# Residual adds ranked over weight tiles, a norm's scale asked for later, and split weights in half tiles: a change to a two-layer decoder trunk

## The chip, the cores and the metric

The kernel runs on one core of one Trainium2 chip. The core has five engines that run side by side: TensorE (PE in the profile; its weight loads are the row PEld), VectorE (DVE), ScalarE (ACT), GpSimd (POOL) and SyncE (SP), which issues most DMA transfers. The metric is the device time of one execution in microseconds, lower being better. The kernel before took 2509.03 us (median of three runs, 2508.16 to 2511.75).

## The reference

The program computes two residual layers over 256 positions of width 2048, in float32. The first layer mixes with a state-space part (SSD) and latent attention (MLA), the second with stick-breaking attention. Each is followed by a gated feed-forward network (FFN) with 5632 hidden columns.

```
def rms_norm(x, g):
    y = x * rsqrt(mean(x * x, axis=-1) + 1e-6)
    return y * g

def swiglu_ffn(h, w_gate, w_up, w_down):
    return (silu(h @ w_gate) * (h @ w_up)) @ w_down

for layer in range(2):
    h = rms_norm(x, mix_norm[layer])
    if layer % 2 == 0: mix = ssd_mla_mixer(h, w_in, ..., w_out)
    else:              mix = stick_breaking_mixer(h, w_qkv, w_out)
    x = x + mix
    x = x + swiglu_ffn(rms_norm(x, ffn_norm[layer]), w_gate[layer], w_up[layer], w_down[layer])
return rms_norm(x, final_norm)
```

All weights are read once from HBM, about 450 MB.

## The kernel before

**Products in three terms.** A float32 operand is split into a rounded part (hi, or wh for weights) and the rest (lo, wl). A product of 128 rows by 512 columns over 128 of K is three matmuls: hi by wh, hi by wl, lo by wh. `split` (L247 to L250) makes the two parts: ScalarE casts (L249), then VectorE subtracts (L250), so wl always comes after wh.

**Weights.** A raw weight tile `w` holds four K blocks of 512 columns (1 MB) and comes by one DMA or a few. `load_split` (L300) walks a weight matrix in groups of four K blocks: it loads the group, then splits it into `wh` and `wl`. Up to the fifth group the split is cut finer (`step`), then a group is one cast and one subtraction. `wh` and `wl` have two buffers each of their own (`whtile`, `wltile`, `wtile` with own=2); in the FFN every third one lies in a region of memory that the two kinds of layer share. Raw tiles have three buffers, and every fourth one in the FFN lies in that shared region.

**The shared region.** `region(kind)` closes the pool that is open and opens another over the same memory. In the attention layers ("acts") it holds 20 small tiles `s2x`, among them the attention outputs that the output projection reads. In the FFN ("sums") it holds one raw tile, two weight sums `wsum`, and one wh and one wl tile. A tile of the new pool waits for the tiles of the old pool that lie where it lies.

**Projections.** `project` (L333) runs all of K for 512 output columns and both tiles of 128 rows, with the matmuls at L340 to L342; K is 2048 in most, that is 16 blocks, four groups. `add_residual` (L390) then adds the result from PSUM to the residual `xres` on VectorE, one instruction per row tile (L395). PSUM has four accumulator banks, two per projection.

**The FFN.** `pair` (L467) computes 512 columns of gate and up together. Over the first half of K it forms seven products instead of eight, out of sums and differences of blocks: the weights' sums t1 to t4 (`wadd`, L464) are made on VectorE, and each of the seven weight operands b11, b22, t1, b21, t2, t4, t3 is then split. The products' matmuls are at L493, L494 and L498, in the order b11, b22, t1, b21, t2, t4, t3. Their left operands (`block_operands`) come from the residual's first two blocks of 512 columns. The second half of K is plain (L526 to L528, in `unit`) and reads the transposed third and fourth blocks. At its end `left` applies Silu, which needs the norm's scale `rstd`, and `right` multiplies. Eleven pairs come in groups of 2, 2, 2, 2, 3; each group is followed by four down projections.

**The norm.** The gain goes into the transposed operand, and the scale 1/rms is applied to results. `norm_block` and `operand_block` transpose one block of 512 columns of the residual on TensorE (L259, L413), finish the operands on ScalarE and VectorE (L268, L270), and square and sum. They run as tasks: a generator that yields counts of ticks; `tick` is called between groups of matmuls and advances those due. `join` runs a task to its end at once. `norm_end` (L383) joins all four blocks, then computes `rstd` by one reduction, six small VectorE instructions and a Sqrt on ScalarE. In `ffn` it is called at L572, ahead of the first pair.

**What sets the order.** TensorE runs in the order of the program text. The other engines' instructions are put in order by a planner that takes, of those ready in its own simulated time, the one with the lowest number; that order is then fixed, and each engine works through it. The default number is 10000000. Weight work counts up from 100000 (`wprio`), so earlier tiles come first, and `URGENT` is 50000. The residual adds have the default number.

The functions that the diff touches, and what calls them:

Of the kernel before, what the change touches and what calls it, by code (L numbers as in the profile page):

```python
# [8 lines left out]
F32 = mybir.dt.float32  # L9
# [6 lines left out]
P = 128  # L16
# [11 lines left out]
class Trunk:  # L28
# [6 lines left out]
    def __init__(self, ctx, tc, ins, out):  # L35
# [13 lines left out]
        self.banks = ["acc0", "acc1", "acc2", "acc3"]  # L49
        self.n, self.wn = 0, {}  # L50
        self.now, self.tasks = 0, []
# [36 lines left out]
    def region(self, kind):  # L88

        if self.shared is not None:  # L90
            self.shared.__exit__(None, None, None)
        self.shared, self.shared_kind = None, kind
        if kind:
            bufs = 20 if kind == "acts" else 2
            self.shared = self.tc.tile_pool(name=f"shared_{kind}", bufs=bufs, reuse_waits="tile")
            self.xp = self.shared.__enter__()
# [4 lines left out]

    def wtile(self, tag="w", dt=F32, bufs=4, own=3):

        n = self.wn[tag] = self.wn.get(tag, 0) + 1
        if self.shared_kind == "sums" and n % bufs == 0:
            return self.xp.tile([P, 4, 512], dt, name=self.nm(tag), tag=tag, bufs=1)
        return self.wp.tile([P, 4, 512], dt, name=self.nm(tag), tag=tag, bufs=own)

    def whtile(self):
        return self.wtile("wh", F32R, 3, 2)  # L110

    def wltile(self):
        return self.wtile("wl", F32R, 3, 2)

# [185 lines left out]
    def load_split(self, view, nk, n):  # L300

        nc = self.nc
        for k0 in range(0, nk, 4):
            k1 = min(nk, k0 + 4)
            res = []
            with self.priority(self.wprio):
# [5 lines left out]
                for ins in self.first if self.wprio <= 105000 else ():  # L312
                    order.enter_context(self.tc.issue_after(ins))
                wh, wl = self.whtile(), self.wltile()
                step = 1 if self.wprio < 102000 else 2 if self.wprio < 106000 else k1 - k0
                for c in range(0, k1 - k0, step):
                    d = c + step
                    self.split(wh[:, c:d, :n], wl[:, c:d, :n], w[:, c:d, :n])
                order.close()
                for k in range(k0, k1):  # L320
                    res.append((wh[:, k - k0, :n], wl[:, k - k0, :n]))
            yield from res
# [67 lines left out]
    def add_residual(self, ps, j, scale=None):  # L390
        nc, x = self.nc, self.xres
        for t in range(2):
            xs = x[:, t, j * 512:(j + 1) * 512]
            if scale is None:
                nc.vector.tensor_tensor(xs, ps[t], xs, op=ALU.add)  # L395
            else:
                nc.vector.scalar_tensor_tensor(xs, ps[t], scale[:, t:t + 1], xs, op0=ALU.mult, op1=ALU.add)

# [55 lines left out]
    def wsplit(self, w):  # L454
        wh, wl = self.whtile(), self.wltile()
        with self.priority(self.wprio):
            self.wprio += 100
            self.split(wh, wl, w)
        return wh, wl
# [90 lines left out]
    def ffn(self, layer, st, gain_next):  # L550
# [83 lines left out]
    def stick(self, st):  # L634
# [82 lines left out]
    def even(self, st):  # L717
# [58 lines left out]
        for n in range(4):  # L776
            ps = self.project(aT, self.cols(wo, n * 512, r0=SSD_W), KD)
            self.add_residual(ps, n)
            (self.operand_block if n < 2 else self.norm_block)(st, n, self.g_ffn[0])
        return st  # L780
# [345 lines left out]
```

## Time and profile before

| | us |
|---|---|
| median of three runs | 2509.03 (2508.16 to 2511.75) |
| the profiled execution's own time | 2512.09 |
| its span, first to last instruction | 2510.4 |
| TensorE busy | 2454.1 (98%) |
| VectorE busy | 1714.3 (68%) |
| ScalarE busy | 1298.1 (52%) |
| GpSimd busy | 130.9 (5%) |

The span is that of the one execution that the hardware profiler recorded; durations that are quoted come from it. A line of a timeline gives the start, the time, the engine, the line of the kernel, the operation, what is written and read, the shapes and the count; in brackets stands how long the engine was idle before it, and what ended that. A matmul of 512 columns shows some 0.39 us, but matmuls overlap and start some 0.23 us apart. The layers lie as follows: the first attention layer to 641 us, its FFN to about 1322, the stick-breaking layer to 1779, its FFN to the end.

### The profile page before, as it was taken

To read this page: it belongs to the slowest core of one execution; us is meant where nothing else is said; L and a number is where in the kernel's file an instruction comes from. 1 tells how busy PE (TensorE), PEld (TensorE's weight loads), DVE (VectorE), ACT (ScalarE), POOL (GpSimd) and SP (SyncE) were. 2 spreads that over 40 slices of the span, in tenths; PEclk is the share of its full clock that TensorE was granted. 3 is DMA by queue.
4 is the path that set the end of the run, shared out by engine and by line. 5 is a ranking of instruction groups with operands and counts; after the bars stand their busy time and mean duration, and the time that the engine had idled before them with its cause. 6 is when DMAs were issued, how large, how long until landed. Compare 5 with 4: busy or idle time off the path is not lost.

```text
span 2510.4 us, 27612 instructions
## 1 busy us (share of the span) xinstructions
PE 2454.1 (98%) x11176; PEld 2008.4 (80%) x11176; DVE 1714.3 (68%) x1476; ACT 1298.1 (52%) x1266; POOL 130.9 (5%) x164
## 2 busy tenths in 40 slices
PE   8999999999899999999999999999899999999998
PEld 7788877788688888888878787778688888888876
DVE  5775455456778778787965444445787878787874
ACT  6655555434554545454544545554554545454553
POOL 1231121000000000000000000000000000000001
PEclk9999999999899999999999999999999999999999
DMA  7654553355555556565554454445555656565653
GB/s 234 194 176 159 178 157 111 126 193 185 182 197 199 194 196 206 184 203 185 204 190 143 166 172 160 151 155 173 181 200 184 217 172 215 170 231 168 235 188 114
DMA packets 257824, 454.78 MB, mean 181 GB/s; under 512 B 20716, under 2 KB 45424, under 8 KB 257696
## 3 DMA queue, kind: packets, MB, share of 16 engines
q1 hardware_dynamic: 255168, 446.48, 53.1%
q0 software_dynamic: 1952, 5.48, 0.6%
q8 instruction: 88, 1.44, 0.2%
q10 hardware_dynamic: 576, 1.05, 0.1%
q14 instruction: 40, 0.33, 0.0%
HBM read 450.85 MB, written 2.13 MB: 180 GB/s over the span
## 4 chain that ended last, share of the span: by engine, by line
PE 56%; issue 39%; ACT 2%; DVE 1%; POOL 0%; DMA 0%; SPq 0%; POOLq 0%; ACTq 0%; DVEq 0%
PE acc L341 11%; PE acc L340 11%; PE acc L342 11%; PE acc L527 3%; PE acc L526 3%; PE acc L528 3%; PE acc L493 3%; PE acc L494 3%; PE acc L498 3%; PE tr L259 1%; ACT wh L249 1%; DVE wl L250 1%; PE at L1049 1%; PE at L978 1%; PE at L1048 0%
## 5 line engine op out<-in xcount | busy, mean ns | idle before, releaser
L250 DVE TENSOR_TENSOR wl<-w,wh 128x2048 fp32r<-128x2048 f32 (+2 forms) x431 | 966.3, 2250 | 578.3 <-ACT wh L249 569.5
L249 ACT CAST wh<-w 128x2048 fp32r<-128x2048 f32 (+2 forms) x431 | 807.3, 1875 | 732.5 <-PE acc L342 414.8
L340 PE MATMUL acc<-wh,s 128*128 128x512 f32 (+1 forms) x1728 | 692.2, 401 | 3.3 <-ACT wh L249 3.3
L341 PE MATMUL acc<-wl,s 128*128 128x512 f32 (+1 forms) x1728 | 673.6, 390 | 7.0 <-DVE wl L250 6.9
L342 PE MATMUL acc<-wh,s 128*128 128x512 f32 (+1 forms) x1728 | 674.2, 390 | 0.0
L341 PEld LDWEIGHTS acc<-wl,s 128*128 128x128 f32 x1728 | 326.2, 189 | 74.4 <-DVE wl L250 10.3
L342 PEld LDWEIGHTS acc<-wh,s 128*128 128x128 f32 x1728 | 325.3, 188 | 70.2
L340 PEld LDWEIGHTS acc<-wh,s 128*128 128x128 f32 x1728 | 325.9, 189 | 67.6 <-ACT wh L249 4.1
L528 PE MATMUL acc<-wl,s 128*128 128x512 f32 x704 | 275.3, 391 | 0.0
L527 PE MATMUL acc<-wh,s 128*128 128x512 f32 x704 | 275.2, 391 | 0.0
L526 PE MATMUL acc<-wh,s 128*128 128x512 f32 x704 | 275.2, 391 | 0.0
L493 PE MATMUL acc<-wh,s 128*128 128x512 f32 x616 | 246.4, 400 | 0.0
L494 PE MATMUL acc<-wh,s 128*128 128x512 f32 x616 | 242.4, 393 | 0.0
L249 ACT CAST wh<-wsum 128x2048 fp32r<-128x2048 f32 x66 | 125.9, 1910 | 84.6 <-PE acc L527 35.7
L498 PE MATMUL acc<-wl,s 128*128 128x512 f32 x616 | 166.1, 391 | 0.0
L250 DVE TENSOR_TENSOR wl<-wsum,wh 128x2048 fp32r<-128x2048 f32 x66 | 150.6, 2285 | 13.8 <-ACT wh L249 13.8
L527 PEld LDWEIGHTS acc<-wh,s 128*128 128x128 f32 x704 | 132.2, 188 | 29.1
L526 PEld LDWEIGHTS acc<-wh,s 128*128 128x128 f32 x704 | 132.2, 188 | 29.0
L528 PEld LDWEIGHTS acc<-wl,s 128*128 128x128 f32 x704 | 132.1, 188 | 29.0
L493 PEld LDWEIGHTS acc<-wh,s 128*128 128x128 f32 x616 | 116.9, 190 | 25.6
L494 PEld LDWEIGHTS acc<-wh,s 128*128 128x128 f32 x616 | 117.0, 190 | 24.3
L498 PEld LDWEIGHTS acc<-wl,s 128*128 128x128 f32 x616 | 115.8, 188 | 25.7
(246 smaller groups left out, 2063.3 us busy)
## 6 DMA issues: line engine op xcount, KB each, us to landing
w<-in_w_gate_dram SPq DMA_DIRECT2D x88, 1024.0 KB, 5.1
w<-in_w_up_dram SPq DMA_DIRECT2D x88, 1024.0 KB, 5.1
w<-in_w_down_dram SPq DMA_DIRECT2D x88, 1024.0 KB, 5.0
w<-in_w_qkv_dram SPq DMA_DIRECT2D x48, 1024.0 KB, 5.0
w<-in_w_in_dram SPq DMA_DIRECT2D x47, 1024.0 KB, 5.2
w<-in_w_out_even_dram SPq DMA_DIRECT2D x32, 1024.0 KB, 4.9
w<-in_w_out_odd_dram SPq DMA_DIRECT2D x16, 1024.0 KB, 5.0
w<-in_w_ukv_dram SPq DMA_DIRECT2D x32, 256.0 KB, 4.1
```

The source lines that it names most:

```text
L249: nc.scalar.copy(hi, src)
L250: nc.vector.tensor_tensor(lo, src, hi.bitcast(F32), op=ALU.subtract)
L259: self.nc.tensor.transpose(pt[:, k, t * P:(t + 1) * P], src(t, 2 * k2 + k), self.ident)
L340: nc.tensor.matmul(ps[t], hi[:, ts], wh, start=k == 0, stop=False)
L341: nc.tensor.matmul(ps[t], hi[:, ts], wl, start=False, stop=False)
L342: nc.tensor.matmul(ps[t], lo[:, ts], wh, start=False, stop=k == nk - 1)
L493: mm(ps, hi[:, k], wh[:, k], start=start and k == 0, stop=False, skip_group_check=True)
L494: mm(ps, lo[:, k], wh[:, k], start=False, stop=False, skip_group_check=True)
L498: mm(ps, hi[:, k], wl[:, k], start=False, stop=k == 3, skip_group_check=True)
L526: mm(ps, hi, wh, start=False, stop=False, skip_group_check=True)
L527: mm(ps, lo, wh, start=False, stop=False, skip_group_check=True)
L528: mm(ps, hi, wl, start=False, stop=stop, skip_group_check=True)
```

## The change

Three things are changed.

1. `add_residual` gives its VectorE instructions the number `URGENT`. The norm blocks of the third and fourth residual block after an output projection get that rank for their operands too.
2. `ffn` no longer calls `norm_end` ahead of the first pair. `left` calls it when it first needs the scale, at the end of that pair's plain part.
3. `wh` and `wl` lie in the shared region alone. In the FFN each has three buffers of four K blocks, as before in number. In the attention layers each has four buffers of two K blocks, and a group of four is split in two halves, each with its own cast and subtraction. Raw tiles stay as they were. The sizes in total are unchanged.

```
     def region(self, kind):
...
         if kind:
-            bufs = 20 if kind == "acts" else 2
-            self.shared = self.tc.tile_pool(name=f"shared_{kind}", bufs=bufs, reuse_waits="tile")
+            self.shared = self.tc.tile_pool(name=f"shared_{kind}", bufs=2, reuse_waits="tile")
             self.xp = self.shared.__enter__()
...
-    def wtile(self, tag="w", dt=F32, bufs=4, own=3):
-
-        n = self.wn[tag] = self.wn.get(tag, 0) + 1
-        if self.shared_kind == "sums" and n % bufs == 0:
-            return self.xp.tile([P, 4, 512], dt, name=self.nm(tag), tag=tag, bufs=1)
-        return self.wp.tile([P, 4, 512], dt, name=self.nm(tag), tag=tag, bufs=own)
-
-    def whtile(self):
-        return self.wtile("wh", F32R, 3, 2)
-
-    def wltile(self):
-        return self.wtile("wl", F32R, 3, 2)
+    def wtile(self):
+
+        self.wn += 1
+        pool, bufs = (self.xp, 1) if self.shared_kind == "sums" and self.wn % 4 == 0 else (self.wp, 3)
+        return pool.tile([P, 4, 512], F32, name=self.nm("w"), tag="w", bufs=bufs)
+
+    def part(self, tag):
+
+        nk, bufs = (2, 4) if self.shared_kind == "acts" else (4, 3)
+        return self.xp.tile([P, nk, 512], F32R, name=self.nm(tag), tag=tag, bufs=bufs)
...
                 for ins in self.first if self.wprio <= 105000 else ():
                     order.enter_context(self.tc.issue_after(ins))
-                wh, wl = self.whtile(), self.wltile()
-                step = 1 if self.wprio < 102000 else 2 if self.wprio < 106000 else k1 - k0
-                for c in range(0, k1 - k0, step):
-                    d = c + step
-                    self.split(wh[:, c:d, :n], wl[:, c:d, :n], w[:, c:d, :n])
+                np = 2 if self.shared_kind == "acts" else 4
+                for a in range(k0, k1, np):
+                    b = min(k1, a + np)
+                    wh, wl = self.part("wh"), self.part("wl")
+                    step = 1 if self.wprio < 102000 else np
+                    for c in range(0, b - a, step):
+                        d = min(c + step, b - a)
+                        self.split(wh[:, c:d, :n], wl[:, c:d, :n], w[:, a - k0 + c:a - k0 + d, :n])
+                    for k in range(a, b):
+                        res.append((wh[:, k - a, :n], wl[:, k - a, :n]))
                 order.close()
-                for k in range(k0, k1):
-                    res.append((wh[:, k - k0, :n], wl[:, k - k0, :n]))
...
             xs = x[:, t, j * 512:(j + 1) * 512]
-            if scale is None:
-                nc.vector.tensor_tensor(xs, ps[t], xs, op=ALU.add)
-            else:
-                nc.vector.scalar_tensor_tensor(xs, ps[t], scale[:, t:t + 1], xs, op0=ALU.mult, op1=ALU.add)
+            with self.priority(self.URGENT):
+                if scale is None:
+                    nc.vector.tensor_tensor(xs, ps[t], xs, op=ALU.add)
+                else:
+                    nc.vector.scalar_tensor_tensor(xs, ps[t], scale[:, t:t + 1], xs, op0=ALU.mult, op1=ALU.add)
...
     def wsplit(self, w):
-        wh, wl = self.whtile(), self.wltile()
+        wh, wl = self.part("wh"), self.part("wl")
...
         def left(t, c, s):
+            nonlocal rstd
+            if rstd is None:
+                rstd = self.norm_end(st)
             nc.vector.tensor_tensor(s, c, s, op=ALU.subtract)
...
             for n in range(n0, n0 + nb):
-                if rstd is None:
-                    rstd = self.norm_end(st)
                 self.pair(st, xT, self.cols(wg, n * 512), self.cols(wu, n * 512), left, right)
...
             self.add_residual(ps, n)
-            (self.operand_block if n < 2 else self.norm_block)(st, n, self.g_ffn[1])
+            if n < 2:
+                self.operand_block(st, n, self.g_ffn[1])
+            else:
+                self.norm_block(st, n, self.g_ffn[1], rank=self.URGENT)
```

The last hunk stands in `stick`; the same one stands in `even`, with `self.g_ffn[0]`.

More of the change, by code (lines that the diff above doesn't have):

```diff
@@ L49, in __init__ @@
         self.banks = ["acc0", "acc1", "acc2", "acc3"]
-        self.n, self.wn = 0, {}
+        self.n = self.wn = 0
         self.now, self.tasks = 0, []
@@ L778, in even @@
             self.add_residual(ps, n)
-            (self.operand_block if n < 2 else self.norm_block)(st, n, self.g_ffn[0])
+            if n < 2:
+                self.operand_block(st, n, self.g_ffn[0])
+            else:
+                self.norm_block(st, n, self.g_ffn[0], rank=self.URGENT)
         return st
```

## The prediction, made before the changed kernel was run

> **What bounds the kernel now.** I read the page's head first, then TensorE's waits, then the windows around the places where it waits, then the order of the instructions there.
>
> ```profile
> span 2510.4 us, 27612 instructions
> PE 2454.1 (98%) x11176; PEld 2008.4 (80%) x11176; DVE 1714.3 (68%) x1476; ACT 1298.1 (52%) x1266; POOL 130.9 (5%) x164
> ```
>
> TensorE is busy for 2454.1 of 2510.4 us; the change adds and removes no matmul, so all that it can win lies in the 56 us in which TensorE is idle, and in what such pauses cost afterwards. TensorE's waits say whom it waits for (us in total, times, longest):
>
> ```profile
> PE tr L259 <- DVE xres L395: 22.7, 2, 11.4
> PE acc L341 <- DVE wl L250: 8.7, 6, 1.8
> PE acc L340 <- ACT wh L249: 4.3, 5, 1.1
> ```
>
> The first row is two pauses of 11.4 us: transposes wait for a residual add. The next two, 13.0 us, are matmuls waiting for the two halves of a split weight tile. The windows around the two long pauses (first two rows), around the four worst waits for weights, all in the stick-breaking layer (next four), and of the two attention layers as a whole:
>
> ```profile
> core 0: us, PE busy (x) PEld busy (x) DVE busy (x) ACT busy (x) POOL busy (x), PEclk, DMA share, GB/s
> 638.00:662.00 24.00, 12.65 (x50) 10.05 (x49) 20.42 (x17) 10.84 (x15) 0.00 (x0) 0.72 0.42 141
> 1776.00:1800.00 24.00, 12.54 (x52) 10.00 (x51) 21.05 (x19) 11.36 (x15) 0.00 (x0) 0.79 0.41 143
> 1437.00:1450.00 13.00, 10.53 (x43) 8.46 (x42) 9.35 (x12) 9.99 (x15) 0.00 (x0) 0.87 0.49 158
> 1516.00:1530.00 14.00, 11.16 (x54) 9.27 (x53) 9.81 (x13) 11.54 (x16) 0.00 (x0) 1.00 0.53 178
> 1594.00:1606.00 12.00, 9.12 (x37) 7.32 (x36) 8.79 (x11) 10.51 (x15) 0.00 (x0) 0.87 0.46 161
> 1675.00:1690.00 15.00, 12.12 (x52) 9.87 (x50) 9.63 (x13) 11.02 (x16) 0.00 (x0) 0.89 0.52 176
> 0.00:640.00 640.00, 630.88 (x3060) 513.34 (x3061) 375.71 (x543) 331.83 (x447) 102.16 (x138) 1.00 0.53 171
> 1322.00:1778.00 456.00, 444.85 (x2030) 366.51 (x2029) 228.33 (x203) 230.43 (x270) 18.91 (x16) 0.99 0.49 163
> ```
>
> TensorE is idle for 11.35 and 11.46 us in the first two, and for 2.47 + 2.84 + 2.88 + 2.88 = 11.1 us in the next four. The granted clock falls too: in three of the four short windows it is 0.87, 0.87 and 0.89, which is 13 x 0.13 + 12 x 0.13 + 15 x 0.11 = 4.9 us of full clock lost. So the weight waits of that layer cost 11.1 + 4.9 = 16.0 us, and they are as large a prize as one and a half of the long pauses.
>
> **The FFN's start (scale asked for later, add ranked first).** TensorE at the first FFN, with the first plain matmul of the pair (L526) and the second pair's stretch for comparison:
>
> ```profile
> 640.71 0.40 PE L342 MATMUL acc<-wh,s2x 128*128 128x512 f32 x1
> ...
> 652.79 1.76 PE L259 MATMUL tr<-ident,xres 128*128 128x128 f32 x7 [11.28 <-DVE xres L395]
> ...
> 675.00 0.39 PE L526 MATMUL acc<-wh,s 128*128 128x512 f32 x1
> ...
> 696.93 0.40 PE L493 MATMUL acc<-wh,s 128*128 128x512 f32 x1
> ...
> 717.12 0.39 PE L526 MATMUL acc<-wh,s 128*128 128x512 f32 x1
> ```
>
> A pair's seven products, with the eight transposes that fall among them, take 717.12 - 696.93 = 20.2 us when nothing waits. With the scale no longer asked for ahead of the pair, TensorE can go on at 640.94, where the project's last matmul gives way. Without any wait the first L526 would then start at 640.94 + 20.2 = 661.1, which is 13.9 us before 675.00. That is the most that can be had here. VectorE's order at the same place says how much of it is real:
>
> ```profile
> 637.49 2.29 DVE L250 TENSOR_TENSOR wl<-w,wh 128x2048 fp32r<-128x2048 f32 x1 [3.27 <-ACT wh L249]
> 640.43 0.69 DVE L395 TENSOR_TENSOR xres<-acc,xres 128x512 f32<-128x512 f32 x1 [0.65 <-PE acc L342]
> 641.04 2.28 DVE L464 TENSOR_TENSOR wsum<-w,w 128x2048 f32<-128x2048 f32 x1
> 643.24 2.28 DVE L250 TENSOR_TENSOR wl<-w,wh 128x2048 fp32r<-128x2048 f32 x1
> ...
> 652.05 0.68 DVE L395 TENSOR_TENSOR xres<-acc,xres 128x512 f32<-128x512 f32 x1
> 652.65 2.28 DVE L464 TENSOR_TENSOR wsum<-wsum,w 128x2048 f32<-128x2048 f32 x1
> 654.85 1.65 DVE L270 SCALAR_TENSOR_TENSOR s<-tr,va,s 128x256 fp32r<-128x256 f32 x4
> ...
> 667.97 0.68 DVE L509 TENSOR_TENSOR s<-s,s 128x512 f32<-128x512 f32 x1
> 668.57 4.48 DVE L250 TENSOR_TENSOR wl<-w,wh 128x2048 fp32r<-128x2048 f32 x2
> ```
>
> The add of the second row tile (652.05) stood behind five pieces of the pair's own weight work, from 641.04 on. They are not wasted: they are the weight sum t1, the split of b22, t2, t3 and the split of t1, and TensorE used them after the pause. Take the pause away and TensorE needs them at once. Rank puts both adds first: 640.43 and about 641.15, done at 641.85. From there VectorE owes, until the first L526 can use its weights: t1, b22, t2, t3, t1's split, t4, b21, t2's split, t4's split, t3's split and the first plain tile: eleven pieces at a pitch of 2.20 us (641.04 to 643.24) = 24.2 us, the last block's four L270 (1.65) and one ranked subtraction (0.6). 641.85 + 26.45 = 668.3. L526 needs only the rounded part, its third matmul needs the rest 0.45 us later, so the pair's plain part runs as if from 667.85: a gain of 675.00 - 667.85 = 7.15 us, not 13.9. The missing 6.7 us come back as short waits of the products (L493, L498) for wh and wl.
>
> What bounds it: if the sums' buffers come free earlier than the project's end, t1 is made before 640.43 and 2.2 us more are won; VectorE has the room, since it waits 3.27 us ahead of 637.49. If the first split (637.49, ahead of the end now) must wait until the old layer's buffers under it are free, 2.2 us go, since the change moves wh and wl into memory that the region before used otherwise. At both starts that is 7.15 - 2.2 to 13.9 each; I take 7 and 7, nearest to the row-by-row sum, hence 14. From these I take 2 for a slower clock after the remaining waits (the three slowed windows above lose 4.9 / 3 = 1.6 us each; half of that at two places is 1.6, rounded up): **12 us**.
>
> On that clock the Trainium skill ("TensorE: Matmul & The Clock Gate", section "What's actually happening") says that it halves only after an idle window of about 3.4 us. By that rule the short waits left here would cost no clock, and the sum would be 2 us lower. This trace differs: the rows at 1437, 1594 and 1675 show the clock below 0.9 with less than 2.9 us idle in each, so I keep the 2 us.
>
> The scale itself moves to the end of the first pair: one reduction, six small VectorE instructions, a Sqrt with its table load on ScalarE, no DMA. They gate the first Silu, and behind that only h's transposes in the next pair. The cover is the pair's plain part, 696.93 - 675.00 = 21.9 us of matmuls that need none of it. Uncovered, they would cost the table load and a few small instructions, some 3 us. The SP queue is passed by nothing. I cost it at 0.
>
> **Weights split in halves in the attention layers.** The second of the four places, on ScalarE, then on VectorE, then on TensorE:
>
> ```profile
> 1513.60 0.53 ACT L691 ACTIVATE s<-s 128x384 f32<-128x384 f32 x1 [2.24 <-POOL s L689]
> 1514.15 0.53 ACT L692 ACTIVATE s<-s 128x384 f32<-128x384 f32 x1
> 1514.70 1.28 ACT L699 ACT_TABLE_LOAD   x1
> ...
> 1518.48 1.90 ACT L249 CAST wh<-w 128x2048 fp32r<-128x2048 f32 x1
> ```
>
> ```profile
> 1520.41 2.29 DVE L250 TENSOR_TENSOR wl<-w,wh 128x2048 fp32r<-128x2048 f32 x1 [0.89 <-ACT wh L249]
> ```
>
> ```profile
> 1520.43 0.49 PE L340 MATMUL acc<-wh,s 128*128 128x512 f32 x1 [1.01 <-ACT wh L249]
> 1522.76 0.50 PE L341 MATMUL acc<-wl,s 128*128 128x512 f32 x1 [1.83 <-DVE wl L250]
> ```
>
> ScalarE waits 2.24 us for GpSimd, loads a table, does the logarithms, and the weight cast queued behind them starts at 1518.48, too late by about 3 us. A four-block tile lasts 24 matmuls at 0.23 us (640.94 - 640.71), 5.5 us. With two buffers a split can start when the tile two before it is used up and has 5.5 us until TensorE wants it; cast and subtraction take 1.90 + 2.29 = 4.2, which leaves 1.3 us. Halves last 2.75 us; with four buffers a half has 3 x 2.75 = 8.25 us. Its price, from the start of the kernel, where tiles are already cut so:
>
> ```profile
> L250 DVE TENSOR_TENSOR wl<-w,wh 128x1024 fp32r<-128x1024 f32 x8 | 9.5, 1221 | 1.3 <-ACT wh L249 1.2
> L249 ACT CAST wh<-w 128x1024 fp32r<-128x1024 f32 x8 | 8.1, 1052 | 0.9 <-DMA w<-in_w_in_dram 0.8
> ```
>
> 1.05 + 1.22 = 2.3 us, which leaves 6 us of slack where there were 1.3. A delay of 3 us is swallowed. The four waits should go: 16.0 us. One wait of the same kind in the latent attention belongs to the 13.0 us of waits; four places take some 11.1, the others hold 1.9, of which I count 1. I take off 1 for what an order made anew may leave: **16 us**. Bounds: 0 if ScalarE's order leaves the halves behind the logarithms, and 17.
>
> More instructions: from the code, 160 groups lie in these layers, all but the first five now whole tiles. Each becomes two, 2 x 1.052 - 1.90 = 0.20 us more on ScalarE and 2 x 1.221 - 2.29 = 0.15 on VectorE, 155 times that is 31 and 23 us. In the 640 + 456 us of these layers ScalarE is busy for 331.83 + 230.43 = 562 us and VectorE for 604, so both have some 500 us free beside TensorE's work: cost 0. With that cover gone, VectorE's 23 us would show. A tile of raw weights is let go 1.9 us earlier (its second half's split is shorter), which only helps the loads.
>
> **The add ranked first everywhere.** 88 adds of 0.69 us move ahead of splits; the quoted add already waits 0.65 us for TensorE at the head of its queue. Split tiles stand three deep in the FFN, so 0.65 + 1.3 us per pair of adds is hidden by a tile of 5.5 us: 0.
>
> **Sum.** 2512.09 us is the profiled execution's own time; minus 12 and 16 gives 2484. The median of the three runs is 2509.03, 3.1 below that execution; the timed result should stand by it: **2481 us**.
>
> **The rivals.**
> - *The FFN waits go entirely* (VectorE gets its head start before the project ends): 27 us of clock and wait instead of 12, 2509 - 27 - 16 = 2466. For it: VectorE idles 3.27 us ahead of 637.49. Against: t1 and b22's split both follow the project's end at once. Chance 0.14.
> - *VectorE gives nothing back at the FFN*: the products wait as long as the transposes did, gain 2; 2509 - 2 - 16 = 2491. For it: VectorE is busy 20.42 of 24 us there. Against: between 656.5 and 667.97 there stand only three pieces of 2.2 us and the scale's small ones. Chance 0.13.
> - *Halves don't cure the waits*, since the order of ScalarE is fixed and GpSimd late: 2509 - 12 - 2 = 2495. Chance 0.12.
> - *Slower: the ranked adds block VectorE.* It runs its queue in order; an add at the head holds all splits until TensorE ends a project. 36 FFN adds in pairs, each 0.65 + 1.3 us; if half of that reaches TensorE's weights, 36 x 0.98 = 35 us, against a gain of 28: 2516. It decides from 0.8 us per pair of adds on. Against: at 640.43 the wait is 0.65 and splits stand ahead. Chance 0.06.
> - *It does nothing that can be seen*, gains and small losses meeting: 2509. Chance 0.04.
>
> **How the numbers follow.** The forecast has 0.51, with its own range 2473 to 2488. The range of 8 in 10 takes in the first three rivals' middles: 2464 to 2498. Within 0.2% is within 5 us, about what a measurement of this kernel can tell from no change; the chances from the cases are 0.90 faster, 0.04 same, 0.06 slower.
>
> **What will show it.** The wait of L259 for L395 is gone, and in its place L493 and L498 wait for L249 and L250 by 5 to 7 us per FFN; the first L526 stands 26 to 28 us behind the last project's end. In the stick-breaking layer L341 waits no longer for L250 and the clock holds 1.00. L250 has some 300 rows of 128x1024. I am wrong if L493 waits for nothing, if L340 still waits behind L699, or if L340 of the down projections waits for wl.

## The result, and the profile after

The changed kernel takes 2533.36 us (median of four runs, 2530.6 to 2536.18) against 2508.88 us (2508.16 to 2511.75) for the kernel before. The ratio is 1.0095, with a 95% interval of 1.0078 to 1.0113. It is 24 us slower, where 2481 us were forecast. (The kernel before now has four runs, hence 2508.88 and not 2509.03.) The profiled execution took 2536.18 us. In the experiments further down the kernel before was run again beside the others, with medians of 2512.08 to 2514.00 us, so runs are compared by their ratios to it. The head of the page of the changed kernel:

```profile
span 2534.5 us, 28070 instructions
PE 2490.0 (98%) x11176; PEld 2011.8 (79%) x11176; DVE 1743.4 (69%) x1631; ACT 1322.6 (52%) x1421; POOL 124.5 (5%) x164
```

TensorE runs the same 11176 matmuls and is busy for 2490.0 us instead of 2454.1. That is 35.9 us more for the same work, while the span grew by 24.1. So TensorE waits less than before, and the matmuls themselves have become slower. First the waits. TensorE's in the changed kernel (us in total, times, longest):

```profile
PE acc L500 <- DVE wl L248: 10.8, 5, 3.3
PE tr L257 <- DVE s L571: 8.4, 4, 2.1
PE at L979 <- POOL s L976: 6.4, 3, 2.1
...
PE acc L342 <- DVE wl L248: 1.9, 2, 1.7
...
PE acc L341 <- ACT wh L247: 0.6, 1, 0.6
```

The two pauses of 11.4 us for the residual add are gone, and of the 13.0 us of waits for split weights in projections 2.5 are left. New are the first row (the FFN's products wait for the rest wl, as foreseen), the third (the SSD part waits for GpSimd), and a larger second one, which stood at 4.3 us before. The windows of the changed kernel, with the columns as in the prediction: the four places in the stick-breaking layer, which lie 18 to 27 us later now, the first 640 us, the stretch that stood at 1322 to 1778 us before, and the start of either FFN.

```profile
1461.00:1474.00 13.00, 13.00 (x64) 10.86 (x63) 10.58 (x16) 12.18 (x19) 0.00 (x0) 1.00 0.56 184
1538.00:1552.00 14.00, 14.00 (x69) 11.87 (x68) 12.63 (x18) 12.72 (x20) 0.00 (x0) 1.00 0.53 177
1612.00:1624.00 12.00, 12.00 (x57) 9.91 (x56) 9.40 (x14) 11.94 (x19) 0.00 (x0) 1.00 0.52 174
1690.00:1705.00 15.00, 15.00 (x74) 12.71 (x73) 13.00 (x19) 13.27 (x22) 0.00 (x0) 1.00 0.52 184
...
0.00:640.00 640.00, 625.46 (x2998) 504.57 (x2999) 390.83 (x630) 341.50 (x534) 104.74 (x138) 0.99 0.53 168
...
1345.00:1788.00 443.00, 441.32 (x2027) 363.04 (x2026) 233.72 (x266) 238.70 (x334) 9.85 (x16) 1.00 0.50 166
...
655.00:685.00 30.00, 24.34 (x95) 18.57 (x94) 29.96 (x24) 20.89 (x22) 0.00 (x0) 0.89 0.35 112
1789.50:1819.50 30.00, 24.70 (x95) 18.90 (x94) 29.96 (x24) 20.87 (x21) 0.00 (x0) 0.89 0.45 145
```

In the four places TensorE is never idle now, and the row of the longer stretch says the same: it is idle for 1.68 of 443 us, where it was 11.15 of 456. In the first 640 us, though, TensorE is busy for 625.46 instead of 630.88. In the last two rows VectorE is busy for all but 0.04 us of 30.

Now the matmuls. Two stretches of TensorE's timeline, in the middle of a down projection where nothing waits, the kernel before first and the changed kernel second. In either, 24 matmuls lie between the first and the last row:

```profile
899.89 0.39 PE L340 MATMUL acc<-wh,s 128*128 128x512 f32 x1
...
905.33 0.39 PE L340 MATMUL acc<-wh,s 128*128 128x512 f32 x1
```

```profile
899.93 0.39 PE L341 MATMUL acc<-wh,s 128*128 128x512 f32 x1
...
905.53 0.39 PE L341 MATMUL acc<-wh,s 128*128 128x512 f32 x1
```

(905.33 - 899.89) / 24 = 226.7 ns before and (905.53 - 899.93) / 24 = 233.3 ns after. Same operation, same shapes, the clock granted in full. The groups of instructions, 512 columns alone, show which matmuls are concerned (busy us, then mean ns of one), the kernel before first:

```profile
L342 PE MATMUL acc<-wh,s 128*128 128x512 f32 x1696 | 665.2, 392 | 0.0
...
L342 PE MATMUL acc<-wh,s2x 128*128 128x512 f32 x256 | 101.5, 397 | 0.0
```

```profile
L343 PE MATMUL acc<-wh,s 128*128 128x512 f32 x1696 | 671.8, 396 | 0.0
...
L343 PE MATMUL acc<-wh,s2x 128*128 128x512 f32 x256 | 99.9, 390 | 0.0
```

Those with an operand in an `s` tile went from 392 to 396 ns; those with an operand in an `s2x` tile, at the same line of the code, from 397 to 390. The pace hangs on which tile is read beside which. What changed there is the place of the tiles. From the addresses that the built program gives to its tiles (bytes inside a partition):

| tiles | bytes, before | bytes, after |
|---|---|---|
| most wh, wl | 62272 and up (own buffers) | 154048 and up (shared region) |
| one wh, wl in three, in the FFN | 186816 and up (shared region) | with all the others |
| operands `s` | 95040 and up | 62272 and up |
| operands `s2x` | shared region | shared region |

What a matmul reads of a tile begins a whole multiple of 256 bytes behind the base, so that only the bases count. Modulo 256, before: own wh and wl 64, `s` 64, shared region 192. After: `s` 64, shared region 192, and all wh and wl are there. So before, two thirds and more of the matmuls read weights and operand a multiple of 256 bytes apart ("in step" below), and after, all but those with `s2x` read them an odd multiple of 128 apart.

The pace by class, from the starts of neighbouring matmuls of 512 columns that are 200 to 262 ns apart (some 9080 of 9816; the rest stand next to a wait or another operation): before, 227.69 ns for 6388 in step and 232.3 to 232.8 ns for 2701 out of step, 229.16 in the mean; after, 227.23 ns for 715 in step and 233.00 for 8356 out of step, 232.54 in the mean. 9816 x (232.54 - 229.16) = 33.2 us. That is more than the whole loss.

Where the waits went was added up by place, as the time by which neighbouring starts on TensorE are further apart than is usual for the same two lines; it includes what a lower clock costs:

| place | before, us | after, us |
|---|---|---|
| four places of the stick-breaking layer | 16.8 | 2.3 |
| one split in the latent attention (325 us) | 1.7 | 0 |
| the two FFN starts | 27.4 | 18.8 |
| transposes behind the first pair of either FFN | 0 | 6.5 |
| transposes in the last pair of either FFN | 6.6 | 8.0 |
| SSD part, three times | 2.6 | 12.5 |
| first projection of the stick-breaking layer | 0 | 2.1 |
| whole kernel | 79.9 | 73.8 |

So the waits shrank by 6.1 us and the pace costs 33.2: 27.1 us, against 24.1 between the two spans; 3 us of this sum are not accounted for. Two things had to be settled by runs: that the offset of the tiles is the cause of the pace, and why the waits shrank by 6 us and not by 28.

### The profile page after: what moved, and what is told of

It reads as the page before. It is cut to its first block, busy times and chain, and to the rows that moved or that the text cites. A ratio compares the mean times of both kernels' runs of the same rounds, so it can differ in the third digit from the quotient of the medians.

```text
span 2534.5 us, 28070 instructions
## 1 busy us (share of the span) xinstructions
PE 2490.0 (98%) x11176; PEld 2011.8 (79%) x11176; DVE 1743.4 (69%) x1631; ACT 1322.6 (52%) x1421; POOL 124.5 (5%) x164
## 3 DMA queue, kind: packets, MB, share of 16 engines
q10 hardware_dynamic: 576, 1.05, 0.1%
## 4 chain that ended last, share of the span: by engine, by line
PE 94%; DVE 3%; issue 1%; POOL 1%; ACT 1%; DMA 0%; SPq 0%; DVEq 0%; POOLq 0%; ACTq 0%
PE acc L341 18%; PE acc L343 18%; PE acc L342 18%; PE acc L529 6%; PE acc L528 6%; PE acc L530 6%; PE acc L500 5%; PE acc L495 5%; PE acc L496 5%; PE tr L257 1%; DVE wl L248 1%; PE at L1058 1%; POOL s L963 1%; PE tr L281 1%; PE at L987 1%
## 5 line engine op out<-in xcount | busy, mean ns | idle before, releaser
L248 DVE TENSOR_TENSOR wl<-w,wh 128x1024 fp32r<-128x1024 f32 (+2 forms) x586 | 999.2, 1711 | 583.0 <-ACT wh L247 575.9
L247 ACT CAST wh<-w 128x1024 fp32r<-128x1024 f32 (+2 forms) x586 | 834.5, 1426 | 831.0 <-PE acc L343 468.6
L530 PE MATMUL acc<-wl,s 128*128 128x512 f32 x704 | 278.2, 395 | 0.0
L529 PE MATMUL acc<-wh,s 128*128 128x512 f32 x704 | 278.1, 395 | 0.0
L528 PE MATMUL acc<-wh,s 128*128 128x512 f32 x704 | 278.0, 395 | 0.0
L495 PE MATMUL acc<-wh,s 128*128 128x512 f32 x616 | 250.5, 407 | 0.0
L496 PE MATMUL acc<-wh,s 128*128 128x512 f32 x616 | 245.1, 398 | 0.0
L500 PE MATMUL acc<-wl,s 128*128 128x512 f32 x616 | 171.8, 400 | 11.0 <-DVE wl L248 10.8
L500 PEld LDWEIGHTS acc<-wl,s 128*128 128x128 f32 x616 | 116.6, 190 | 41.7 <-DVE wl L248 14.0
L495 PEld LDWEIGHTS acc<-wh,s 128*128 128x128 f32 x616 | 117.9, 191 | 28.4
```

Of the source, the lines that this page charges most:

```text
L247: nc.scalar.copy(hi, src)
L248: nc.vector.tensor_tensor(lo, src, hi.bitcast(F32), op=ALU.subtract)
L495: mm(ps, hi[:, k], wh[:, k], start=start and k == 0, stop=False, skip_group_check=True)
L496: mm(ps, lo[:, k], wh[:, k], start=False, stop=False, skip_group_check=True)
L500: mm(ps, hi[:, k], wl[:, k], start=False, stop=k == 3, skip_group_check=True)
L528: mm(ps, hi, wh, start=False, stop=False, skip_group_check=True)
```

## The experiments on the pace

Theory: a 512-column matmul is slower whenever the tile that streams through (wh, wl) and the one that is loaded as weights of the array (the operand) aren't a multiple of 256 bytes apart. Rival: the changed code, with its halves and its 310 more instructions on ScalarE and VectorE beside the matmuls, makes them slower. The tool is an unused stretch of memory behind the operands' tiles and ahead of the shared region, which moves all tiles there and alters no instruction and no order. In the changed kernel:

```
-        self.kpeT = self.small([P, S], "kpeT", bufs=1)
+        self.kpeT = self.small([P, S + 96], "kpeT", bufs=1)[:, :S]
```

**384 bytes in the changed kernel.** 128 + 384 is 512, two times 256.

> The changed kernel with 384 bytes of unused memory ahead of the shared region, and nothing else; the order of every engine's instructions stays the same. Theory A (byte offset): TensorE's pace depends on whether the weight tile that streams and the operand tile that is loaded start at the same offset within 512 bytes. In the changed kernel nearly all weight tiles lie in the shared region, whose start is 128 bytes off the operands' tiles; matmuls start 233.0 ns apart there and 227.7 ns where offsets agree. With the shift all agree: 9912 matmuls x 5 ns = 50 us less, 2533 - 50 = 2484 us. Theory B (new waits and the finer splits' own traffic slow TensorE, wherever the tiles lie): no change, 2533 us. Theory C (the upper part of memory is slow): no change, 2533 us.

2492.82 us (2491.44 to 2498.28), ratio to the kernel before 0.9922 (0.9907 to 0.9936). All timed matmuls are in step, at 227.29 ns. That is short of the 2484 us expected: TensorE's busy time on the page fell by 54 us from 2490.0, with the same instructions, but its idle time grew from 44.5 to 53.8 us (its waits for wl in the FFN and for GpSimd went from 10.8 and 6.4 to 14.0 and 10.1 us):

```profile
PE 2435.9 (98%) x11176; PEld 2005.3 (81%) x11176; DVE 1739.1 (70%) x1631; ACT 1324.8 (53%) x1421; POOL 127.5 (5%) x164
...
L343 PE MATMUL acc<-wh,s 128*128 128x512 f32 x1696 | 663.4, 391 | 0.0
```

**128 bytes in the changed kernel** (`S + 32`), so that the offset is 256 and not 512.

> The changed kernel with 128 bytes of unused memory ahead of the shared region: its tiles then start 256 bytes off the operands' tiles within 512. Theory A with 512 bytes as the unit: still out of step, 2533 us, pace 232 to 233 ns. Theory A with 256 or 128 bytes as the unit: 256 gives full pace, 2484 us; 128 is ruled out by the changed kernel itself. Theories B and C: 2533 us.

2495.53 us, ratio 0.9924 (0.9908 to 0.9941), pace 227.24 ns. 256 bytes are as good as 512.

**384 bytes in the kernel before** (the same line there), which moves its shared region into step with its own buffers.

> The kernel before with 384 bytes of unused memory ahead of the shared region. There 2700 of 9100 timed matmuls have one operand in the shared region and start 232.5 ns apart, the others 227.7. Theory A: 2701 x 4.9 ns over 9089 timed of 9912 matmuls, 14 us less, 2495 us. Theories B and C: 2509 us.

2495.96 us, ratio 0.9931 (0.9916 to 0.9946), pace 227.26 ns. The line costs nothing and gives the kernel before 0.7%, with none of the change in it. It also shows what the change's own edits are worth once the pace is the same: 0.9922 against 0.9931, which the intervals don't tell from nothing.

**128 bytes ahead of the operands' tiles in the kernel before**, which puts it out of step:

```
+        nc.gpsimd.memset(self.ap.tile([P, 32], F32, name="pad", tag="pad", bufs=1), 0.0)
```

> The kernel before, with an unused tile of 128 bytes allocated ahead of its tiles for operands, so that nearly all weight tiles and operand tiles (8384 of 9089 matmuls that the trace times) come to lie an odd multiple of 128 bytes apart; none of the change's edits. Theory (the offset of 128 bytes costs each 512-column matmul about 5 ns of 227, whatever the rest of the code): the pace of nearly all goes to 232 to 233 ns, and the time to about 2509 + 33 = 2542 us, the changed kernel's slow pace without its edits. Rival (the slower pace of the changed kernel belongs to its edits, to halves and to more instructions beside the matmuls, and the padding of the earlier runs cured it by something else): 2509 us, the pace as before, 229 ns in the mean.

2543.94 us (2543.12 to 2545.9), ratio 1.0115 (1.0098 to 1.0132). 8377 of the 9081 timed matmuls are out of step, at 232.9 to 233.2 ns; the other 704 take 227.0. The page and the groups of this kernel, 512 columns alone:

```profile
PE 2488.9 (98%) x11176; PEld 2012.5 (79%) x11176; DVE 1719.1 (68%) x1476; ACT 1300.7 (51%) x1266; POOL 125.0 (5%) x165
...
L343 PE MATMUL acc<-wh,s 128*128 128x512 f32 x1696 | 671.5, 396 | 0.0
...
L343 PE MATMUL acc<-wh,s2x 128*128 128x512 f32 x256 | 100.4, 392 | 0.0
```

2488.9 us of TensorE, within 1.1 us of the changed kernel's 2490.0, from the kernel before with one unused tile and one memset. That excludes the rival: no edit of the change is needed for the slower pace, and with all its edits in place the pace of 227 ns is there as soon as the tiles are moved.

It also excludes that the place of one of the two tiles alone decides. Weights at 64 modulo 256 are quick in the kernel before (operands at 64) and slow here (operands at 192); operands at 64 are quick in the kernel before and slow in the changed one.

**64 and 32 bytes out of step in the changed kernel** (`S + 80` and `S + 88`), to see whether small offsets do less harm.

> The changed kernel with 80 bytes of padding, so that weights and operands lie 64 bytes out of step. Known so far: 0 and 256 bytes 227.3 ns, 128 and 384 bytes 232 to 233 ns. If the pace falls off with the distance in proportion: about 230 ns and 2515 us. If only whole multiples of 256 are good: 232 to 233 ns and 2533 us. If the unit is something below 128 bytes, 227 ns and 2493 us (which the slow pace at 128 bytes speaks against).

> The changed kernel with 88 bytes of padding, so that weights and operands lie 32 bytes out of step. In proportion to the distance: about 228.6 ns and 2503 us. If only whole multiples of 256 are good: 232 to 233 ns and 2533 us. If small distances cost nothing: 227.3 ns and 2493 us.

2536.74 and 2535.97 us, one run each; the pace out of step is 233.29 and 233.22 ns. There is no part of the way: 32 bytes out of step cost as much as 128. What the chip does in these 5 to 6 ns isn't shown by any run, nor whether the tile that streams gets in the way of the operand under work or of the next one's load, since the two had the same offset in every matmul that was timed.

## The experiments on the waits

**Parts 1 and 2 alone** (the ranked adds, and the scale asked for later) in the kernel before; weights are neither halved nor moved.

```
+            with self.priority(self.URGENT):
                 if scale is None:
...
+            if rstd is None:
+                rstd = self.norm_end(st)
             nc.vector.tensor_tensor(s, c, s, op=ALU.subtract)
...
-                if rstd is None:
-                    rstd = self.norm_end(st)
```

> The kernel before with the residual adds and the third and fourth norm blocks ranked first and the scale asked for at the end of the first pair; weights and their buffers as before. Theory A: what the changed kernel lost is due to where its tiles lie and not to these two edits; they gain what the trace shows at the two FFN starts, 27.4 us of excess before and 18.8 after, so 2509 - 9 = 2500 us. Rival: the two edits bring waits of their own (transposes waiting for the gated product in the first and second FFN, 6 us in the changed kernel) and gain 2 us, 2507, or lose.

2509.31 us (ten runs, 2502.35 to 2511.53), ratio 0.9986 (0.9977 to 0.9996): some 3.5 us won, where the theory asked for 9 and the rival for 2. The clearest mark of the FFN start is the time from the end of the project ahead to the first plain matmul of the pair. It fell from 34.06 and 33.43 us (first and second FFN) to 28.34 and 27.42, which is 11.7 us. So some 8 us were given back elsewhere, and TensorE's waits show a part of it:

```profile
PE tr L259 <- DVE s L570: 9.1, 4, 2.6
...
PE acc L499 <- DVE wl L250: 6.5, 2, 3.3
...
PE acc L494 <- ACT s L505: 3.1, 2, 1.6
```

The first row is the one that stood at 4.3 us, so 4.8 us of the 8 are in it; where the rest went was not followed up. (The other two rows lie inside the FFN starts.) Two of the first row's four waits are new, and both stand in the second pair: transposes of h wait for the gated product, which is late on VectorE. A pair's work on VectorE is no shorter for being begun sooner, and what TensorE gains at the start of the first pair it loses in part in the second.

**The changed kernel without the rank** (the tiles in step, as in all runs that follow here; `add_residual` and the norm blocks as before the change).

> The changed kernel with the shift of 384 bytes (2492.8 us), and the residual adds and the norm blocks' operands at their old rank; scale still asked for late, weights in halves. Theory V (the ranked add stands at the head of VectorE's queue for 7.9 us, with the first split of the pair behind it): the first wait of L500, 3.7 us at each FFN's start, and the 2.1 us at the start of the stick-breaking layer go, but the fourth block's transposes, which now fall in the first product, wait for the adds behind the pair's weight work, some 8 us at each start: 2492.8 - 9.5 + 16 = 2499 us. Rival: the rank decides nothing, 2493 us.

2500.24 us, ratio 0.9954 (0.9939 to 0.9969), against 0.9922 with the rank: the rank is worth some 8 us. TensorE's waits bring the old row back:

```profile
PE tr L257 <- DVE xres L396: 24.9, 2, 12.5
...
PE acc L499 <- DVE wl L248: 5.4, 2, 2.7
```

Two of the expectations failed. The first wait for wl at each FFN start did not go; it is 2.7 us in the second row (line L499 here, L500 with the rank). The wait at the first projection of the stick-breaking layer stayed too (1.69 us), so the rank isn't its cause.

**Whole tiles in the first attention layer, halves only in the stick-breaking layer.** The number of K blocks in a tile becomes a variable, with as many bytes in buffers as before; the first five groups are cut finer again, as in the kernel before.

```
-        nk, bufs = (2, 4) if self.shared_kind == "acts" else (4, 3)
+        nk, bufs = (self.np, 8 // self.np) if self.shared_kind == "acts" else (4, 3)
...
-        oT, xT, rstd = [], self.pairs(st["xT"]), None
+        oT, xT, rstd, self.np = [], self.pairs(st["xT"]), None, 2
```

> The changed kernel with the shift of 384 bytes, but whole tiles of four K blocks with two buffers in the first attention layer, halves only in the stick-breaking layer. Theory H (the halves' casts push the state-space part's Exp on ScalarE and with it GpSimd's products back, so that TensorE waits for GpSimd three times, 3.5 us and 1.5 us of slow clock each): 15 us less, and 1.7 us more for the one wait in latent attention: 2492.8 - 13 = 2480 us. Rival: these waits come from the ranked adds or from where tiles lie: 2493 us.

2478.97 us (2478.23 to 2483.5), ratio 0.9871 (0.9857 to 0.9886), 13 us better than with halves everywhere. The window of the SSD's three groups, in the kernel before, the changed kernel, the changed kernel with its tiles in step, and this one (columns as before):

```profile
130.00:250.00 120.00, 120.00 (x593) 98.62 (x592) 80.29 (x135) 68.04 (x79) 33.33 (x26) 1.00 0.51 168
```

```profile
130.00:250.00 120.00, 113.59 (x537) 90.81 (x536) 83.36 (x143) 66.10 (x89) 37.24 (x27) 0.97 0.47 151
```

```profile
130.00:250.00 120.00, 109.90 (x520) 88.00 (x520) 78.42 (x136) 64.91 (x86) 40.17 (x27) 0.96 0.45 149
```

```profile
130.00:250.00 120.00, 120.00 (x593) 98.62 (x592) 80.25 (x135) 68.14 (x79) 33.35 (x26) 1.00 0.52 168
```

TensorE never waits there with whole tiles, before or now. With halves it is idle for 6.4 us, or 10.1 once the matmuls are quicker, and the clock drops besides: 120 x 0.04 = 4.8 us in the third row. Neither the rank nor the place of the tiles is the cause: without the rank the waits for GpSimd were 10.1 us as well, and the last row has the rank and the tiles in step. How it comes about is seen on ScalarE, GpSimd and TensorE around 140 us, first before and then after the change:

```profile
137.22 1.67 ACT L953 ACTIVATE s<-s 128x512 f32<-128x512 f32 x3
...
137.93 4.00 POOL L954 TENSOR_TENSOR s<-s,s 128x512 f32<-128x512 f32 x3 [1.80 <-ACT s L953]
141.90 3.15 POOL L967 TENSOR_TENSOR s<-s2x,edec 128x512 f32<-128x512 f32 x1
```

```profile
138.26 0.63 ACT L962 ACTIVATE s<-s 128x512 f32<-128x512 f32 x1
138.80 1.03 ACT L247 CAST wh<-w 128x1024 fp32r<-128x1024 f32 x1
139.73 1.67 ACT L962 ACTIVATE s<-s 128x512 f32<-128x512 f32 x3
...
138.97 1.36 POOL L963 TENSOR_TENSOR s<-s,s 128x512 f32<-128x512 f32 x1 [16.10 <-ACT s L962]
141.10 2.21 POOL L994 TENSOR_TENSOR s2x<-s2x,s 128x512 f32<-128x512 f32 x1 [0.76 <-DVE s L993]
143.26 5.75 POOL L963 TENSOR_TENSOR s<-s,s 128x512 f32<-128x512 f32 x3
148.97 1.04 POOL L976 TENSOR_TENSOR s<-s2x,edec 128x512 f32<-128x512 f32 x1
...
150.07 1.55 PE L979 MATMUL at<-s,s 128*128 128x512 f32 x2 [2.14 <-POOL s L976]
```

The exponentials of a group feed a chain on GpSimd, and at its end stands the product that TensorE wants. Halves make twice as many casts and subtractions, all with a lower number than the SSD's own work, and the planner sets them between its pieces: here a cast lies between the exponentials. GpSimd begins a group's four products 13 us later than before (the first of them had run at 125.6) and ends its chain at 150.0 instead of 145.05, and TensorE stands still from about 148. The chain has another delay in it: its three products in a row take 5.75 instead of 4.00 us here, and VectorE's halves beside them 1.59 to 2.00 us instead of 1.22. The Trainium skill ("GPSIMD Engine Reference", section "1. Specifications") says that GpSimd shares its interfaces to SBUF, the on-chip memory of the tiles, with VectorE, and that VectorE instructions with two inputs there contend. The trace agrees as far as it goes; no run here took the two apart.

**The first split ahead of the adds.** At the FFN's start the changed kernel shows VectorE idle at the head of its queue (VectorE, ScalarE and TensorE of the changed kernel):

```profile
654.62 1.38 DVE L397 TENSOR_TENSOR xres<-acc,xres 128x512 f32<-128x512 f32 x2 [7.89 <-PE acc L343]
655.92 2.28 DVE L466 TENSOR_TENSOR wsum<-w,w 128x2048 f32<-128x2048 f32 x1
658.12 2.28 DVE L248 TENSOR_TENSOR wl<-w,wh 128x2048 fp32r<-128x2048 f32 x1
...
649.86 1.91 ACT L247 CAST wh<-w 128x2048 fp32r<-128x2048 f32 x1 [4.39 <-PE acc L343]
...
660.46 2.07 PE L500 MATMUL acc<-wl,s 128*128 128x512 f32 x4 [3.32 <-DVE wl L248]
```

The first weight's cast is done at 651.77, VectorE has nothing to do, and yet the subtraction comes at 658.12, behind the ranked adds, which wait for TensorE, and behind t1. TensorE then waits 3.32 us for it. Theory: the order on VectorE costs these 3 us or so per FFN. The run takes the last version, makes the first split ahead of t1 and holds the last projection's adds back until it is issued:

```
+        if self.pending:
+            w11 = self.wsplit(b11)
+            with self.tc.issue_after(self.last_lo.ins):
+                self.pending()
+            self.pending = None
```

> As the run with whole tiles in the first attention layer, and at each FFN's start the first pair's first split is traced ahead of its first sum, with the last projection's two adds queued behind that split on VectorE. Theory V: the first split is done before the project ends, the first wait of L500 (3.7 us at each start) goes or shrinks, 2 x 3 us: 2480 - 6 = 2474 us. Rival (VectorE's load after the project's end is what counts, whatever comes first): the wait moves to a later product and 2 x 2.2 us are won at most, 2476 to 2480 us.

2476.81 us (2476.11 to 2481.11), ratio 0.9863 (0.9848 to 0.9877); beside 2478.97 for the version without it, that is not told from nothing. From project end to the first plain matmul it takes 30.21 and 28.50 us, where it took 29.56 and 29.55. The wait has moved on (TensorE, ScalarE and VectorE of this version):

```profile
640.84 0.50 PE L508 MATMUL acc<-wh,s 128*128 128x512 f32 x1 [1.76 <-ACT wh L248]
...
651.75 2.07 PE L513 MATMUL acc<-wl,s 128*128 128x512 f32 x4 [4.54 <-DVE wl L249]
...
638.89 3.71 ACT L248 CAST wh<-w 128x2048 fp32r<-128x2048 f32 x2 [8.74 <-PE acc L343]
...
640.82 2.29 DVE L249 TENSOR_TENSOR wl<-w,wh 128x2048 fp32r<-128x2048 f32 x1 [5.08 <-ACT wh L248]
```

t1 was made early this time, but at the first FFN the casts had to wait 8.74 us for the project's last matmuls, which end at 638.9: the FFN's wh and wl lie where the project's wh, wl and `s2x` operands lie. So the first split was not done before the project ended, though the theory asked for that, and VectorE, with t1 already made, stood idle for 2 us more than in the version without the edit (busy for 28.23 of the 30.20 us from the project's end, against 29.56 of 29.60). At the second FFN the split was done 1.7 us behind the project's end, and the start is 1.05 us sooner. What the order on VectorE costs in the changed kernel, where the cast was done before the project's end, is not shown by this run.

**Two sums less.** The other theory is that VectorE's amount of work sets the start. This run leaves out the sums t3 and t4 of the first pair of either FFN and uses b12 and t2 in their place, so that the output is not the reference's; it has halves everywhere and the tiles in step, as the first run of all.

```
-        t3 = self.wadd(b12, b12, b22)
+        fresh, self.fresh = self.fresh, False
+        t3 = b12 if fresh else self.wadd(b12, b12, b22)
...
-        t4 = self.wadd(self.wsum(), t2, b21)
+        t4 = t2 if fresh else self.wadd(self.wsum(), t2, b21)
```

> The changed kernel with the shift of 384 bytes; the first pair of each FFN leaves out two of its four weight sums (t3 is taken as b12, t4 as t2), so its gate and up values are not the reference's. It takes 2 x 2.2 us off VectorE between the project's end and the first plain matmul. Theory V2 (the waits left at an FFN's start are VectorE's load): the first plain matmul comes up to 4.4 us earlier at each start, 2492.8 - 8 = 2485 us. Rival (TensorE waits for buffers, transposes or data there): 2493 us.

2486.14 us (2481.57 to 2490.69), ratio 0.9902 (0.9883 to 0.9921) against 0.9922. The runs lie far apart, but the mark of the FFN start does not: 25.18 and 25.20 us, where the same kernel with all sums has 29.59 and 29.58. Two pieces of 2.20 us are left out, and the start is 4.4 us sooner, both times. So from the project's end on VectorE's work is the bound there, and each piece counts in full; the 29.96 of 30 us in the windows above say the same.

## Why the prediction was wrong

**The step that failed** is the first inference of the text, that all which the change can win or lose lies in TensorE's idle time because it adds and removes no matmul. Where the third part "moves wh and wl into memory", the text asked only what waits for that memory, 2.2 us per split. It never asked whether the same matmul takes as long with its tiles elsewhere. It did not: +33.2 us by the pace, more than the forecast gain of 28 and of the other sign. The trace of before held the mark: at the same line, the group with `s2x` operands had 397 ns against 392. No rival covered it, and the one rival on the slower side (ranked adds that block VectorE in every project, 2516) is not what happened. Most of what the text said would show it did come (no wait of the transposes for the add, 5.7 and 5.2 us of waits for wl at the two FFN starts, a clock of 1.00 in the stick-breaking layer). Of its three signs of being wrong one came, by the letter: L493, now L495, waits for nothing, since the products wait at L500. All three signs are waits, and the loss is in busy time.

**Halves in the stick-breaking and latent layers: 16 us forecast, 16.2 measured** in the places named (16.8 - 2.3 + 1.7). TensorE no longer waits there, and the clock shows 1.00 in all four windows, as the text said it would in the stick-breaking layer.

**"More instructions: cost 0" failed.** The text set 31 us of ScalarE and 23 us of VectorE against 500 free us in the layers' total, an average over stages. In the SSD's three groups the halves came between pieces of a chain that has no slack, and TensorE lost 9.9 us; 2.1 more went at the first projection of the stick-breaking layer. Whole tiles in the first layer gave 13 us back. The latent attention, in the same layer, lost 1.7 us again with whole tiles.

**The FFN starts: 12 us forecast, 0.7 measured** in the net. The rank does what it was said to do, and the first wait did turn into waits of the products for wl. But from the project's end to the first plain matmul 29.68 us passed, not the 26.9 that 667.85 - 640.94 makes. Of these 2.8 us, some 2.2 are the first split: the sum took it as done ahead of the project's end, as at 637.49 before, and it stands at 658.12, behind the adds and t1. The text named that risk but put it down to memory; here the cast was done at 651.77, and the add at the head of VectorE's queue was in the way. And a step was left out, what is late next. VectorE stays behind by the same work, and the transposes in the second pair wait for the gated product: 6.5 us in two places, 1.4 more in the last pairs. The clock term was taken as 2 us for both. The windows show 0.89 over 30 us, which is 3.3 us for each. No single wait there is above 3.32 us. The words of the Trainium skill ("TensorE: Matmul & The Clock Gate", section "What's actually happening"), by which the clock is halved after an idle window of about 3.4 us, come near to this, but they don't cover the last pairs: there the granted clock was 0.50 for 3.41 us from 1280.45 us on, behind a single wait of 2.10 us.

**The ranked add, "0 everywhere",** holds in the FFN's own down projections, where no new wait appeared. At the two projects ahead of an FFN it does not hold: the add keeps VectorE waiting for 7.89 us with a split ready behind it. By the run with two sums less, a piece of 2.2 us is worth 2.2 us there, so that is some 2.2 us per FFN as an estimate; no run shows it by itself, and in the net the rank gains 8 us.

**The scale, 0:** no trace shows a wait for it. In the changed kernel VectorE's last instruction for it stands at 687.97 us, and the first Silu of the pair, which needs it, at 700.20, behind a product's result of 699.48.

One window of the prediction reached too far: the first FFN's down projections run on to about 1367 us, and not 1322, so the window from 1322 has some 45 us of FFN in it. Its idle time is that of the stick-breaking layer all the same.

## What to carry to other kernels

When a change moves buffers, compare the mean time of the same matmul before and after, by form, before looking at waits; and compare, in one kernel, groups at the same line that read different tiles. Here bases that are equal modulo 256 bytes were worth 17 us to the kernel before and 43 to the changed one (0.7 and 1.7%), for one line of padding. An average of free time over a layer says nothing of a chain inside it, and a wait that ends on a full engine comes back behind the next product.

The version that is quickest of those run has the tiles in step, whole tiles in the first attention layer, halves in the stick-breaking layer, both other parts of the change, and (for no sure gain) the first split ahead: 2476.81 us, 0.9863 of the kernel before.

## What the runs showed of the hardware

That the pace of a matmul hangs on the distance in memory between its two operands was not expected. In numbers, for 128 by 512 float32 matmuls in a stream, from the starts of neighbours:

| distance modulo 256 bytes | ns, start to start | runs |
|---|---|---|
| 0 | 227.0 to 227.7 | before, after (`s2x`), three with padding, 128 bytes ahead of the operands (`s2x`) |
| 128 | 232.3 to 233.2 | before (shared region), after, 128 bytes ahead of the operands |
| 192 | 233.3 | 64 bytes short of a multiple |
| 224 | 233.2 | 32 bytes short of a multiple |

The step is 2.5%, it is there or not there, and it shows in no wait: the engine counts as busy throughout. Whether distances below 32 bytes matter, and whether other shapes or types show it, was not tried.
